# Strassen products for nine pairs of projection units, with GpSimd making the sums

## The chip, the cores and the metric

One core of one Trainium2 chip runs the kernel. The metric is device time in microseconds, the median of the runs. The engines are named as the profile names them: PE (TensorE, matmuls; PEld is its weight load), DVE (VectorE), ACT (ScalarE), POOL (GpSimd) and SP (SyncE, which issues most DMAs). Each engine works through its own instructions in a fixed order, and semaphores hold an instruction until its inputs are there.

## The reference

A decoder layer on 1024 tokens of width 1024, in float32. After a modulated RMS norm, one wide projection feeds a convolution branch and an attention branch.

```python
h = _rmsnorm(x, norm_g[layer]) * (1.0 + scale) + shift
proj = h @ w_in[layer]
(glu_a, glu_b, z_conv, q, k, v, z_att, g_conv, g_att) = jnp.split(proj, split_idx, axis=-1)
u = glu_a * jax.nn.sigmoid(glu_b)
u = lax.conv_general_dilated(u, conv_w...)+ conv_b        # depthwise, causal, 31 taps
u = jax.nn.silu(_layernorm(u, conv_ln_g[layer], conv_ln_b[layer]))
y_conv = (u * jax.nn.silu(z_conv)) @ w_conv_out[layer]
...                                                        # dilated attention on q, k, v
merged = jax.nn.sigmoid(g_conv) * y_conv + jax.nn.sigmoid(g_att) * y_att
x = x + gate * (merged @ w_o[layer])
return _rmsnorm(x, final_g)
```

## The kernel before

Matrices are kept transposed in tiles of 128 channels by 1024 tokens. Every float32 product is made as three matmuls of reduced-precision parts (`mm3`, L73 to L75): a tile is split into a high part, rounded by ScalarE, and a low part, the difference (`split`, L57 and L58). `hh` and `hl` are the two parts of the normed input `h`, resident for the whole projection.

The work goes in stages. A start stage loads and norms, and projects the first `Values` group and three units. Then comes the list `todo`: a `Unit` is one tile of 128 output channels (two halves of 512 tokens, each 8 x 3 matmuls of 128x512 into one PSUM bank), with weights loaded into `wraw` by SP and split into `whi` and `wlo`. A `Values` entry is a group of value columns, as long as four units. Units of the list are the GLU halves of the eight convolution tiles (`Glu(ct)`: sigmoid half, then the half that makes the tile `u`), the SiLU gates `za` of the attention, the SiLU of `z_conv` (kept in the SBUF tiles `z0` to `z7`), and last the eight gate units of the merge (to DRAM).

Beside these matmuls VectorE runs the convolution, one generator `conv(ct, u)` per tile: 31 taps into two accumulators `v` and `v2`, alternately, their sum, and a running sum `tot1` over the tiles. `pump` is a small planner: after each piece of matmuls it hands VectorE as many operations as the piece's cost allows (`PIECE`, `OP`, `HALF`), and `spend` books other VectorE work against it. Outside the two hand-ordered stages (the start and the attention) the framework's scheduler then sets each engine's final order.

At the entry `last_tap` all convolutions must be done (`drain`), and `norm` starts: the mean by a matmul of `tot1` with ones (L534), squares and their sum `tot2`, column sums on TensorE (L127), a row of factors `lrow`, then for each tile the multiplication by `lrow`, SiLU, product with the SiLU of `z`, and the split into `uh` and `ul`. Eight gate units run beside it. Then the output units of the convolution branch (`project` with `uh` and `ul`, L73 `d<-uh,whi`), the attention, the output of attention, and the last projection.

GpSimd does almost nothing until the attention stage, where it makes the low parts of the weights of `q`, `k` and the gates (L58 on POOL).

Of the kernel before, what the change touches and what calls it, by code (L numbers as in the profile page):

```python
# [8 lines left out]
F32 = mybir.dt.float32  # L9
# [7 lines left out]
P = 128  # L17
# [22 lines left out]
def layer(ctx: ExitStack, tc: tile.TileContext, a, out):  # L40
# [58 lines left out]
    bscr = dram.tile([2, 512], F32, name="bscr")  # L99
    cscr = dram.tile([KT, P, S], F32, name="cscr")  # L100
    ascr = dram.tile([KT, P, S], F32, name="ascr")
    gcscr = dram.tile([KT, P, S], F32, name="gcscr")
# [266 lines left out]
    def slot(tag, name, dt=F32, bufs=1):  # L369
        return pb.tile([P, S], dt, name=name, tag=tag, bufs=bufs)  # L370

    def temp(name):
        return slot("tmp", name, bufs=3)

# [20 lines left out]

    tot1 = slot("l0", "tot1")
    v_t = [None] * KT

    def conv(ct, u):
        v = v_t[ct] = slot(f"v{ct}", f"v{ct}")  # L400
        v2 = temp("v2")
        nc.vector.tensor_scalar(v, u[:, 0:S], cw[:, ct, 0:1], cvec[:, 0, ct:ct + 1], op0=mult, op1=add)
        yield HALF
        nc.vector.tensor_scalar(v2, u[:, 1:1 + S], cw[:, ct, 1:2], None, op0=mult)
        yield HALF
        for k in range(2, TAPS):
            d = v2 if k % 2 else v
            nc.vector.scalar_tensor_tensor(d, u[:, k:k + S], cw[:, ct, k:k + 1], d, op0=mult, op1=add)  # L408
            yield OP
        nc.vector.tensor_add(v, v, v2)  # L410
        yield OP
        if ct == 0:
            nc.vector.tensor_copy(tot1, v)
            yield HALF
        else:
            nc.vector.tensor_add(tot1, tot1, v)
            yield OP

# [3 lines left out]
    class Unit:  # L422


        def __init__(self, u, consume, cost=0.0):
            self.u, self.consume, self.cost = u, consume, cost

        def prepare(self):
            spend(OP)
            self.w = weights(a["w_t"][self.u])  # L430

# [14 lines left out]
    class Values:  # L446
# [5 lines left out]
        def prepare(self):  # L452
            self.w = []
            for kp in range(4):
                raw = load_raw(a["w_v"][self.g, kp])
                hi, lo = slot(f"z{kp}", f"vh{kp}", F32R), slot(f"z{4 + kp}", f"vl{kp}", F32R)
                split(hi, lo, raw)
                spend(OP)
                self.w.append((hi, lo))

        def run(self):
            for t in range(8):
# [12 lines left out]
                yield  # L475

    class Glu:

# [3 lines left out]

        def sig(self, half, s, ps):
            if not half:
                self.sb = temp("sigb")
            nc.scalar.activation(self.sb[:, s], ps, AF.Sigmoid)

        def glu(self, half, s, ps):
            if not half:
                self.u = up.tile([P, TAPS - 1 + S], F32, name="u", tag="u", bufs=2)  # L490
                nc.gpsimd.memset(self.u[:, 0:TAPS - 1], 0.0)
            o = TAPS - 1 + half * 512
            nc.vector.tensor_mul(self.u[:, o:o + 512], ps, self.sb[:, s])
            if half:
                behind.append(conv(self.ct, self.u))
# [3 lines left out]

    def to_tile(tiles, n, name, func, make):  # L500
        def consume(half, s, ps):
            if not half:
                tiles[n] = make(name)
            nc.scalar.activation(tiles[n][:, s], ps, func)
        return consume

    sz_t = [None] * KT

    def to_dram(scr, func=AF.Sigmoid):
        def consume(half, s, ps):  # L510
            y = pb.tile([P, 512], F32, name="gs", tag="gs", bufs=2)
            nc.scalar.activation(y, ps, func)
            nc.sync.dma_start(scr[:, s], y)
        return consume

    za = [Unit(40 + j, to_dram(zascr[j], AF.Silu)) for j in range(4)]
    second = Glu(1)
    todo = [second.units()[1], za[0], *Glu(2).units(), Values(1), *Glu(3).units(), *Glu(4).units(), Values(2),
            *Glu(5).units(), *Glu(6).units(), *za[1:], *Glu(7).units()]
    for ct in range(KT):  # L520
        todo.append(Unit(44 + ct, to_tile(sz_t, ct, f"sz{ct}", AF.Silu, lambda n, ct=ct: slot(f"z{ct}", n))))
    last_tap = len(todo)
    for d in range(KT):
        todo.append(Unit(52 + d, to_dram(gcscr[d])))


    ch, cl = [None] * KT, [None] * KT

    def norm():
# [7 lines left out]
        lrow = up.tile([P, TAPS - 1 + S], F32, name="lrow", tag="u", bufs=2)[:, 0:S]  # L537
        tot2 = slot("l0", "tot2")
        for ct in range(KT):
            nc.vector.tensor_sub(v_t[ct], v_t[ct], mean)  # L540
            yield OP
            if ct == 0:
                nc.scalar.activation(tot2, v_t[ct], AF.Square)
            else:
                sq = temp("sq2")
                nc.scalar.activation(sq, v_t[ct], AF.Square)
                nc.vector.tensor_add(tot2, tot2, sq)
                yield OP
# [5 lines left out]
        for half in range(2):  # L554
            half_row(lrow, lcols, half)
        yield PIECE
        for ct in range(KT):
            v = v_t[ct]
            nc.vector.tensor_mul(v, v, lrow)
            yield OP  # L560
            sg_ = temp("sgu")
            nc.scalar.activation(sg_, v, AF.Silu, scale=cvec[:, 1, ct:ct + 1], bias=cvec[:, 2, ct:ct + 1])
            nc.vector.tensor_mul(v, sg_, sz_t[ct])
            yield OP
            hi = slot(f"z{ct}", f"uh{ct}", F32R)
            lo = slot(f"v{ct - 1}" if ct else "l0", f"ul{ct}", F32R)
            split(hi, lo, v)
            yield OP
            ch[ct], cl[ct] = hi, lo

    todo[0].prepare()
    g_ = Glu(0)
# [3 lines left out]
    for n, unit in enumerate(todo):  # L576
        if n + 1 < len(todo):
            todo[n + 1].prepare()
        if n == last_tap:
            drain()  # L580
            behind.append(norm())
        for _ in unit.run():
            pump(PIECE)
    drain()
# [6 lines left out]
    stab = tabs.tile([P, S], F32, name="stab")  # L591
    posi = pb.tile([P, S], I32, name="posi", tag="tmp", bufs=3)
    nc.sync.dma_start(posi, a["positions"].to_broadcast([P, S]))
    n_ = temp("n_")
    nc.vector.tensor_copy(n_, posi)
# [20 lines left out]

    cb = slot(f"v{KT - 1}", "cb")

    def co_load(d):
        sg_ = temp("sgc")  # L620
        nc.sync.dma_start(sg_, gcscr[d])
        return weights(a["w_co"][d]), sg_
# [3 lines left out]
    for d in range(KT):  # L626
# [5 lines left out]
        def gated(half, s, ps):  # L632
            y = pb.tile([P, 512], F32, name="gs", tag="gs", bufs=2)
            nc.vector.tensor_mul(y, ps, sg_[:, s])  # L634
            nc.sync.dma_start(cscr[d][:, s], y)
            if not half:
                modulation(2 * KT + d, gate_c[:, d:d + 1], wa, temp("jk"), cb)

# [652 lines left out]
```

## Time and profile before

| what | us |
|---|---|
| median of 3 runs (1255.39 to 1258.27) | 1258.24 |
| the profiled execution | 1258.8 |
| its span | 1257.0 |
| TensorE busy | 1233.3 |
| VectorE busy | 909.0 |
| ScalarE busy | 511.7 |
| GpSimd busy | 91.5 |

A matmul's record is longer than the step from one to the next, since they are pipelined, so matmul records must not be added up: the step is read from the start times. In the rows of groups, the first number after the bar is the busy time of the group, the second the mean duration of one. In the rows of a timeline, the first number is the start in the span, the second the duration, and "x2" marks two equal neighbours put together.

### The profile page before, as it was taken

How to read it: one execution, taken by the hardware profiler on the slowest of the kernel's cores; microseconds unless marked ns; L12 is line 12 of the kernel's file. 1: busy time of each engine (PE TensorE's matmuls, PEld its weight loads, DVE VectorE, ACT ScalarE, POOL GpSimd, SP SyncE). 2: the span in 40 equal slices, each digit the busy share in tenths (PEclk: the TensorE clock that was granted, in tenths of full speed). 3: DMA queues.
4: the chain of work that ended last, by engine and by line, in shares of the span. 5: the costliest groups of instructions: out<-in, count | busy, mean ns of one | idle time of the engine just before them, and what ended most of it. 6: DMA issues, size and time to landing. Idle time of an engine off the chain costs nothing.

```text
span 1257.0 us, 16947 instructions
## 1 busy us (share of the span) xinstructions
PE 1233.3 (98%) x6208; PEld 1033.5 (82%) x6208; DVE 909.0 (72%) x1496; ACT 511.7 (41%) x1023; POOL 91.5 (7%) x79
## 2 busy tenths in 40 slices
PE   5999999999999999999999999999999999999997
PEld 4877888888888888888888888888888888887886
DVE  6776999999999986873325657777776762448554
ACT  4554202111222135931015656666666665345211
POOL 0000000000000000000031111111111012100000
PEclk9999999999999999999999999999999999999999
DMA  9531311311211112455636555665575563668231
GB/s 362 174 122 59 118 51 59 109 59 51 74 61 51 51 53 82 127 174 193 191 85 150 133 131 145 164 172 144 158 186 146 133 185 120 205 224 294 100 101 67
DMA packets 89751, 165.35 MB, mean 132 GB/s; under 512 B 28547, under 2 KB 42179, under 8 KB 89669
## 3 DMA queue, kind: packets, MB, share of 16 engines
q1 hardware_dynamic: 72992, 157.67, 42.0%
q10 hardware_dynamic: 16676, 6.61, 1.9%
q8 instruction: 49, 0.80, 0.3%
q14 instruction: 34, 0.27, 0.1%
HBM read 105.74 MB, written 27.04 MB: 106 GB/s over the span
## 4 chain that ended last, share of the span: by engine, by line
PE 94%; DMA 2%; DVE 1%; ACT 1%; issue 0%; SPq 0%; ACTq 0%; DVEq 0%
PE d L73 22%; PE d L75 22%; PE d L74 22%; PE o L916 4%; PE t L895 2%; PE d L1195 2%; PE d L1194 2%; PE d L469 2%; PE d L1196 2%; PE d L467 2%; PE d L468 2%; PE s L881 2%; PE s L880 2%; PE d L251 1%; PE d L249 1%; PE d L250 1%
## 5 line engine op out<-in xcount | busy, mean ns | idle before, releaser
L73 PE MATMUL d<-hh,whi 128*128 128x512 f32 x1072 | 421.4, 393 | 0.0
L74 PE MATMUL d<-hl,whi 128*128 128x512 f32 x1072 | 418.4, 390 | 1.9 <-DVE hl L349 1.9
L75 PE MATMUL d<-hh,wlo 128*128 128x512 f32 x1072 | 418.7, 391 | 0.0
L408 DVE SCALAR_TENSOR_TENSOR v<-u,cw,v 128x1024 f32<-128x1024 f32 x232 | 280.6, 1285 | 0.0
L75 PEld LDWEIGHTS d<-hh,wlo 128*128 128x128 f32 x1072 | 201.4, 188 | 42.6
L74 PEld LDWEIGHTS d<-hl,whi 128*128 128x128 f32 x1072 | 201.6, 188 | 41.4 <-DVE hl L349 2.8
L73 PEld LDWEIGHTS d<-hh,whi 128*128 128x128 f32 x1072 | 201.6, 188 | 38.9 <-issue 0.2
L57 ACT ACTIVATE whi<-wraw 128x512 fp32r<-128x512 f32 (+1 forms) x106 | 85.8, 830 | 212.7 <-PE d L74 204.8
L58 POOL TENSOR_TENSOR wlo<-wraw,whi 128x512 fp32r<-128x512 f32 (+1 forms) x56 | 82.1, 1481 | 644.0 <-ACT whi L57 643.9
L884 DVE CUSTOM_DVE_ANT_0 sb<-s,mask 128x128 f32<-128x128 f32 (+1 forms) x192 | 59.9, 350 | 68.3 <-PE s L881 67.7
L888 ACT ACTIVATE sb<-sb,stats 128x128 f32<-128x128 f32 (+1 forms) x192 | 84.9, 444 | 39.0 <-DVE stats L884 38.7
L916 PE MATMUL o<-ph,vt 128*64 128x128 f32 (+1 forms) x432 | 70.9, 270 | 0.0
L895 PE MATMUL t<-ident,sb 128*128 128x128 f32 x280 | 70.8, 274 | 0.0
L58 DVE TENSOR_TENSOR wlo<-wraw,whi 128x1024 fp32r<-128x1024 f32 (+1 forms) x50 | 57.4, 1149 | 14.7 <-ACT whi L57 14.1
L713 ACT ACTIVATE ph<-t 128x384 fp32r<-128x384 f32 (+2 forms) x96 | 45.7, 476 | 37.8 <-PE t L895 31.5
L916 PEld LDWEIGHTS o<-ph,vt 128*64 128x64 f32 x432 | 50.0, 135 | 8.8
L716 DVE TENSOR_TENSOR pl<-t,ph 128x384 fp32r<-128x384 f32 (+2 forms) x96 | 52.0, 542 | 4.2 <-ACT ph L713 3.7
L916 PE MATMUL o<-pl,vt 128*64 128x128 f32 (+1 forms) x216 | 52.9, 261 | 0.0
L1194 PE MATMUL d<-oh,hh 128*128 128x512 f32 (+1 forms) x136 | 51.3, 377 | 0.0
L1196 PE MATMUL d<-oh,hl 128*128 128x512 f32 (+1 forms) x136 | 51.3, 377 | 0.0
L880 PE MATMUL s<-k,q 128*128 128x128 f32 (+1 forms) x192 | 51.1, 291 | 0.0
L634 DVE TENSOR_TENSOR gs<-d,sgc 128x512 f32<-128x512 f32 x16 | 11.1, 692 | 54.9 <-PE d L75 48.9
(227 smaller groups left out, 1909.6 us busy)
## 6 DMA issues: line engine op xcount, KB each, us to landing
wraw<-in_w_t SPq DMA_DIRECT2D x67, 512.0 KB, 3.9
k<-kqp SPq DMA_DIRECT2D x96, 128.0 KB, 2.4
q<-kqp SPq DMA_DIRECT2D x96, 128.0 KB, 2.5
wa<-in_w_ada SPq DMA_DIRECT2D x16, 512.0 KB, 6.6
ql<-kqp SPq DMA_DIRECT2D x48, 128.0 KB, 2.4
wg<-wscr SPq DMA_DIRECT2D x48, 128.0 KB, 3.1
wraw<-in_w_v SPq DMA_DIRECT2D x11, 512.0 KB, 3.6
x<-in_xT SPq DMA_DIRECT2D x8, 512.0 KB, 10.2
```

Of the source, the lines that this page charges most:

```text
L57: nc.scalar.activation(hi, raw, AF.Copy)
L58: (lo_eng or nc.vector).tensor_sub(lo, raw, hi.bitcast(F32))
L73: nc.tensor.matmul(ps, lh, rh, start=start, stop=False)
L74: nc.tensor.matmul(ps, lh, rl, start=False, stop=False)
L75: nc.tensor.matmul(ps, ll, rh, start=False, stop=stop)
L408: nc.vector.scalar_tensor_tensor(d, u[:, k:k + S], cw[:, ct, k:k + 1], d, op0=mult, op1=add)
L880: nc.tensor.matmul(ps[:, c:c + w], q[:, ts_], k[:, ks], start=True, stop=False)
L888: nc.scalar.activation(sb[:, c:c + w], sb[:, c:c + w], AF.Exp, bias=stats[:, t, h, 1:2], scale=-1.0, accum_out=stats[:, t, h, 0:1])
L895: yield from ((lambda c=c: nc.tensor.transpose(ps[:, c:c + P], sb[:, c:c + P], ident)) for c in range(0, o, P))
L916: nc.tensor.matmul(out_, l, r, **kw))
L1194: nc.tensor.matmul(ps, hh[:, k, c], rh, start=k == 0, stop=False)
L1196: nc.tensor.matmul(ps, hl[:, k, c], rh, start=False, stop=k == KT - 1)
```

## The change

Nine times, two units that were made one after the other are made together as a `Pair`. Two units of 128 channels on 1024 tokens with 1024 input channels are a product of 2x2 blocks (input channels in two halves, tokens in two halves, the two units), and Strassen's scheme in Winograd's form makes it with seven block products of 4 x 3 matmuls instead of eight. Four sums of blocks of `h` are needed once (`h_sums`, split into parts, in the SBUF tiles `t0` to `t15`), four sums of weight blocks for each pair, and seven sums of results. GpSimd makes the sums of `h` and of weights and all their low parts, the low parts of `Values` and of the gate units, six low parts of the norm, and the running sum `tot1` for all convolution tiles but the last; VectorE adds the results from PSUM. The first tap of each convolution goes to ScalarE. Convolution tiles that are finished while the sums of `h` occupy SBUF go to DRAM (`put_away`) and come back later (`fetch`); the SiLU of `z_conv` goes to DRAM as well (`szscr`) and is loaded in the norm. The list is in a new order: seven plain units, the nine pairs, then three gates with the two `Values` between them, then `last_tap` and five gates.

```diff
+    def put_away():
+        for ct, v, away in stores:
+            if ct == 0:
+                nc.gpsimd.tensor_copy(tot1, v)
+            else:
+                (nc.gpsimd if ct + 1 < KT else nc.vector).tensor_add(tot1, tot1, v)
+            if away:
+                nc.sync.dma_start(vdr[ct], v)
+                stored.append(ct)
+        stores.clear()
+    def fetch():
+        for ct in stored:
+            v_t[ct] = slot(f"t{8 + ct}", "vb")
+            nc.sync.dma_start(v_t[ct], vdr[ct])
+        stored.clear()
     def conv(ct, u):
-        nc.vector.tensor_scalar(v, u[:, 0:S], cw[:, ct, 0:1], cvec[:, 0, ct:ct + 1], op0=mult, op1=add)
+        nc.scalar.activation(v, u[:, 0:S], AF.Identity, bias=cvec[:, 0, ct:ct + 1], scale=cw[:, ct, 0:1])
         nc.vector.tensor_scalar(v2, u[:, 1:1 + S], cw[:, ct, 1:2], None, op0=mult)
...
         nc.vector.tensor_add(v, v, v2)
-            nc.vector.tensor_add(tot1, tot1, v)
+        stores.append((ct, v, away))
...
     class Values:
-                split(hi, lo, raw)
+                split(hi, lo, raw, nc.gpsimd)
...
+    def h_sums(c):
+        tensor = nc.gpsimd
+        ha, hb = slot("t19", "ha"), slot("t20", "hb")
+        for x, k in ((ha, c), (hb, c + 4)):
+            tensor.tensor_add(x, hh[:, k].bitcast(F32), hl[:, k].bitcast(F32))
+        (a11, a21), (a12, a22) = ((x[:, 0:512], x[:, 512:1024]) for x in (ha, hb))
+        s1, s2, s3, s4 = a22, a11, a21, a12
+        tensor.tensor_add(s1, a21, a22)
+        tensor.tensor_sub(s3, a11, a21)
+        tensor.tensor_sub(s2, s1, a11)
+        tensor.tensor_sub(s4, a12, s2)
+        for i, raw in ((0, s1), (2, s3), (1, s2), (3, s4)):
+            split(sum_tile(i, 0, c), sum_tile(i, 1, c), raw, tensor)
+    class Pair:
+        def prepare(self):
+            tensor = nc.gpsimd
+            ra, rb = (load_raw(a["w_t"][x.u]) for x in self.units)
+            b11, b21, b12, b22 = ra[:, 0:512], ra[:, 512:], rb[:, 0:512], rb[:, 512:]
...
+            split(*w["b11"], b11, tensor)
+            tensor.tensor_sub(t1, b12, b11)
+            tensor.tensor_sub(t3, b22, b12)
+            split(*w["t1"], t1, tensor)
+            tensor.tensor_sub(t2, b22, t1)
+            split(*w["t2"], t2, tensor)
+            split(*w["t3"], t3, tensor)
...
+            split(*w["b21"], b21, tensor)
+            tensor.tensor_sub(t4, b21, t2)
...
+            split(*w["t4"], t4, tensor)
+            split(*w["b22"], b22, tensor)
+        def product(self, ps, name, x):
+            hi, lo = self.w[name]
+            for c in range(4):
...
+                mm3(ps, hi[:, w], lo[:, w], rh, rl, c == 0, c == 3)
+        def run(self):
...
+            nc.scalar.activation(p, product("b11", (0, 0)), AF.Copy)
+            x = product("t2", 2)
+            sums((r, x, p))
+            x = product("t3", 3)
+            sums((q, x, r))
+            x = product("t1", 1)
+            sums((r, x, r))
+            sums((o22, x, q))
+            x = product("b21", (0, 1))
+            sums((p, x, p))
+            one.consume(0, wide(0), p, p)
+            x = product("t4", (1, 1))
+            sums((q, x, q))
+            one.consume(1, wide(1), q, q)
+            x = product("b22", 4)
+            sums((r, x, r))
+            for half, x in ((0, r), (1, o22)):
+                two.consume(half, wide(half), x, x)
...
+gates = [Unit(52 + d, to_dram(gcscr[d]), lo_eng=nc.gpsimd) for d in range(KT)]
+zc = [Unit(44 + ct, to_dram(szscr[ct], AF.Silu)) for ct in range(KT)]
+todo = [second.units()[1], za[0], *Glu(2).units(), *za[1:]]
+for glu, z in ((3, 0), (4, 1), (None, 2), (5, 3), (6, None), (7, None)):
+    if glu:
+        todo.append(Pair(*Glu(glu).units()))
+    if z is not None:
+        todo.append(Pair(*zc[2 * z:2 * z + 2]))
+todo += [gates[0], Values(1), gates[1], Values(2), gates[2]]
 last_tap = len(todo)
+todo += gates[3:]
...
     def norm():
-            split(hi, lo, v)
+            split(hi, lo, v, nc.gpsimd if ct < 6 else None)
...
     for n, unit in enumerate(todo):
+        put_away()
+        if n < 4:
+            h_sums(n)
```

What this does to the order on GpSimd is seen in two pieces. All of GpSimd's work between the start of the projections and the attention was, before, one clearing of the head of `u` per convolution tile; the next row is already the attention's:

```order
L491 MEMSET u 128x30 x8
L58 TENSOR_TENSOR wlo<-wraw,whi 128x8x64 x4
L662 MEMSET ql 64x1024 x3
L670 MEMSET mask 128x256
L671 AFFINE_SELECT mask<-mask 128x128
```

Now 40 operations of `h_sums` stand there first, and then the parts of one pair after another with running sums between them. This is the first pair's piece (`wt` and `wlo` are low parts, L557 to L570 the sums of weight blocks, `tot` the running sum):

```order
L58 TENSOR_TENSOR wt<-wraw,wt 128x512
L647 MEMSET u 128x30
L412 COPY tot_790<-v_850 128x1024
L58 TENSOR_TENSOR wlo<-wraw,whi 128x512
L557 TENSOR_TENSOR wraw<-wraw 128x512
L558 TENSOR_TENSOR wraw<-wraw 128x512
L58 TENSOR_TENSOR wt<-wraw,wt 128x512
L562 TENSOR_TENSOR wraw<-wraw 128x512
L58 TENSOR_TENSOR wt<-wraw,wt 128x512
L570 TENSOR_TENSOR wraw<-wraw 128x512
L58 TENSOR_TENSOR wlo<-wraw,whi 128x512 x4
```

A queue of 158 operations has come to GpSimd ahead of the norm, and a running sum there waits for the last sum of a convolution on VectorE, with the next parts behind it.

On VectorE, before, where the third convolution ends and the fourth begins (L408 are taps, L410 the sum of the two accumulators, L416 the running sum, L402 and L404 the first two taps of the next tile, L493 the product that makes its `u`):

```order
L408 SCALAR_TENSOR_TENSOR v_1388<-u,cw,v_1388 128x1024
L408 SCALAR_TENSOR_TENSOR v_1387<-u,cw,v_1387 128x1024
L402 TENSOR_SCALAR v_1722<-u,cw,cvec 128x1024
L493 TENSOR_TENSOR u<-d,sigb 128x512 x2
L410 TENSOR_TENSOR v_1387<-v_1387,v_1388 128x1024
L404 TENSOR_SCALAR v_1723<-u,cw 128x1024
L416 TENSOR_TENSOR tot_765<-tot_765,v_1387 128x1024
L408 SCALAR_TENSOR_TENSOR v_1722<-u,cw,v_1722 128x1024
```

Now, in the first pair (L601 are the seven sums, with `d` a PSUM bank; L435 and L438 taps; L440 the sum of the two accumulators; L649 the product that makes `u`):

```order
L438 SCALAR_TENSOR_TENSOR v_1196<-u,cw,v_1196 128x1024
L601 TENSOR_TENSOR gs<-d,gs 128x512
L601 TENSOR_TENSOR gs<-d,pq 128x512
L440 TENSOR_TENSOR v_1196<-v_1196,v_1197 128x1024
L601 TENSOR_TENSOR pq<-d,pq 128x512
L431 TENSOR_SCALAR v_1522<-u,cw 128x1024
L435 SCALAR_TENSOR_TENSOR v_1521<-u,cw,v_1521 128x1024
L601 TENSOR_TENSOR pq<-d,pq 128x512
L435 SCALAR_TENSOR_TENSOR v_1522<-u,cw,v_1522 128x1024
L649 TENSOR_TENSOR u<-gs,sigb 128x512
L601 TENSOR_TENSOR gs<-d,gs 128x512
```

The running sum and the first tap have left VectorE's row, as the low parts of the paired units' weights have, and sums that wait for TensorE's products have come in between the taps, in order with them.

180 lines of the change are left out of this document (127 added, 53 removed).

## The prediction

> **What bounds the kernel now.** I read the page's busy times first, then the busy times by stretch, then the chain of work that ended last, then the groups of instructions inside the stretch that the change rewrites, and last the timelines of VectorE and GpSimd where both work.
>
> ```profile
> PE 1233.3 (98%) x6208; PEld 1033.5 (82%) x6208; DVE 909.0 (72%) x1496; ACT 511.7 (41%) x1023; POOL 91.5 (7%) x79
> ...
> core 0: us, PE busy (x) PEld busy (x) DVE busy (x) ACT busy (x) POOL busy (x), PEclk, DMA share, GB/s
> 0.00:101.78 101.78, 86.95 (x376) 68.98 (x377) 70.08 (x97) 53.22 (x56) 0.85 (x7) 1.00 0.59 210
> 101.78:460.56 358.78, 358.78 (x1584) 297.26 (x1583) 353.37 (x312) 72.78 (x94) 4.19 (x8) 1.00 0.20 66
> 460.56:552.37 91.81, 91.81 (x414) 75.68 (x413) 70.51 (x71) 61.14 (x67) 0.00 (x0) 1.00 0.35 111
> 552.37:1257.00 704.63, 695.80 (x3837) 591.53 (x3835) 415.04 (x1017) 324.56 (x807) 86.44 (x64) 1.00 0.56 156
> ```
>
> The four stretches are: the start; the projections with the convolution beside them; the layer norm of the convolution beside the gate units; the rest. TensorE is never idle in the second and third, and its clock is granted in full (1.00). The second holds 1584 matmuls in 358.78 us, 0.2265 us each, and the chain steps in the same beat (a matmul's own record is longer, because they overlap):
>
> ```profile
> 300.05 0.23 PE d L74
> 300.27 0.23 PE d L75
> 300.50 0.23 PE d L73
> ```
>
> But VectorE is busy for 353.37 of those 358.78 us: the two engines are level there, and GpSimd does nothing. What fills VectorE in that stretch, and two rows from later stages that I need for prices:
>
> ```profile
> L408 DVE SCALAR_TENSOR_TENSOR v<-u,cw,v 128x1024 f32<-128x1024 f32 x232 | 280.6, 1285 | 0.0
> L58 DVE TENSOR_TENSOR wlo<-wraw,whi 128x1024 fp32r<-128x1024 f32 x25 | 30.6, 1226 | 2.2 <-ACT whi L57 1.8
> L493 DVE TENSOR_TENSOR u<-d,sigb 128x512 f32<-128x512 f32 x16 | 10.7, 689 | 7.2 <-ACT sigb L486 6.0 <-ACT vh L57 1.1
> L410 DVE TENSOR_TENSOR v<-v,v 128x1024 f32<-128x1024 f32 x8 | 9.8, 1224 | 0.0
> L404 DVE TENSOR_SCALAR v<-u,cw 128x1024 f32<-128x1024 f32 x8 | 6.0, 754 | 0.0
> ...
> L1166 DVE TENSOR_TENSOR sgr<-d,sgr 128x512 f32<-128x512 f32 x16 | 10.6, 686 | 5.4 <-ACT sgr L1151 5.3
> ...
> L562 ACT ACTIVATE sgu<-v,cvec 128x1024 f32<-128x1024 f32 x8 | 9.5, 1238 | 0.1
> ```
>
> The 232 convolution taps alone are 280.6 us, and each reads two SBUF tensors (the input `u` and its own accumulator).
>
> **What VectorE and GpSimd do to each other.** GpSimd works beside VectorE in the attention stage. First GpSimd's rows there, then VectorE's at the same times:
>
> ```profile
> 776.68 2.55 POOL L58 TENSOR_TENSOR wlo<-wraw,whi 128x512 fp32r<-128x512 f32 x2 [14.83 <-ACT whi L57]
> 1006.38 2.38 POOL L58 TENSOR_TENSOR wlo<-wraw,whi 128x1024 fp32r<-128x1024 f32 x1 [17.05 <-ACT whi L57]
> 1087.55 3.04 POOL L58 TENSOR_TENSOR wlo<-wraw,whi 128x1024 fp32r<-128x1024 f32 x1 [8.95 <-ACT whi L57]
> 825.32 2.72 POOL L58 TENSOR_TENSOR wlo<-wraw,whi 128x512 fp32r<-128x512 f32 x2 [11.77 <-ACT whi L57]
> ```
>
> ```profile
> 775.98 0.42 DVE L716 TENSOR_TENSOR vt<-vr,vt 128x256 fp32r<-128x256 f32 x1 [0.25 <-ACT vt L713]
> 777.17 0.87 DVE L943 TENSOR_TENSOR sd<-sd 128x48 f32<-128x48 f32 x1
> 778.08 1.18 DVE L944 TENSOR_TENSOR ma<-sd 128x16 f32<-128x16 f32 x1
> 825.33 0.55 DVE L716 TENSOR_TENSOR pl<-t,ph 128x384 fp32r<-128x384 f32 x1
> 1006.61 2.43 DVE L716 TENSOR_TENSOR vt<-vr,vt 128x256 fp32r<-128x256 f32 x1
> 1087.24 1.08 DVE L979 TENSOR_TENSOR wg<-wg,oc 128x512 f32<-128x512 f32 x1
> 1088.36 2.78 DVE L997 TENSOR_TENSOR wg<-wg 128x512 f32<-128x512 f32 x1
> 1091.18 0.69 DVE L1000 TENSOR_TENSOR wg<-wg,gt 128x512 f32<-128x512 f32 x1
> ```
>
> A product of 128x512 takes 0.69 us at 1091.18; the one at 1088.36 takes 2.78, and ends at 1091.14, 0.55 after the GpSimd operation of 1087.55 (end 1090.59). That operation in its turn began under the VectorE product that ended at 1088.32, and from there on took 2.27 us, as against 2.38 where nothing is in its way. The 0.42 us low part took 2.43 at 1006.61 and ended 0.28 after GpSimd. A sum of 16 columns took 1.18 us beside the second GpSimd operation of 776.68. So an operation of VectorE with two SBUF inputs and one of GpSimd do not run together: whichever came first finishes, the other waits, and they take turns. The low part at 825.33, which reads PSUM and one SBUF tile, took its 0.55 us beside GpSimd: such operations are exempt. The price of a turn is the sum of both, less what overlaps: 2.38 − 2.27 = 0.11 on GpSimd; on VectorE 0.28 instead of the 0.35 that such an operation adds to a busy queue (0.42 less the 0.07 by which a tap's 1.285 us record exceeds its 280.6 / 232 = 1.21), so 0.07. That is 0.18 us a turn.
>
> The Trainium skill, "SBUF — State Buffer", section "SBUF: two separate sides", has this as a rule: VectorE and GpSimd share one port pair as an exclusive lock, taken for the whole instruction by a VectorE operation with two SBUF inputs (or in a two-port mode) or by a GpSimd operation that reads SBUF, and the loser fully blocks. The rows above agree in kind (2.78 us for 0.69); by the rule's whole instructions, without the 0.18 us, the sum below would come to 1452 us, an estimate from that page.
>
> **The change part by part.**
>
> *Matmuls.* Nine pairs, each 7 products of 12 matmuls instead of 96: 9 × 12 = 108 fewer, × 0.2265 = 24.5 us less TensorE work. TensorE alone would reach the mean matmul of the norm (L692) after 7 plain units (336), 9 pairs (756), 3 gates (144), 2 `Values` (384) and 12 more matmuls: 1632 × 0.2265 = 369.6 us, at 471.4.
>
> *VectorE up to there.* 232 taps 280.6; the second tap 6.0; the final sums of two accumulators 9.8; 5 low parts of plain units at 1.22, 6.1; 16 `u` products 10.7; one running sum 1.2; new, 9 × 7 = 63 sums of a product from PSUM with an SBUF tile, at 10.6 / 16 = 0.66 as L1166: 42. Together 356.4 us by group times (the same groups gave 363 before, of which 353.4 were busy time, since neighbours overlap): the first taps (to ScalarE), 28 low parts and 7 running sums go, 63 sums come. VectorE's first operation there comes at about 105. Alone it would end at 461.5, ahead of TensorE.
>
> *GpSimd up to there.* Counted in its new order: 131 operations of 128x512 (32 in the sums of `h`, 99 in the pairs) and 27 of 128x1024 (8 sums of `h`, 7 running sums, 12 low parts of gates and `Values`). At 2.55 / 2 = 1.27 and 2.38: 166.4 + 64.3 = 230.7 us. (The first running sum is a copy; its price is not shown, between the nothing of a copy that locks no one out and 2.38; I take the upper end, since it moves the sum by less than 1%.)
>
> *How they add.* If they exclude each other: 105 + 356.4 + 230.7 = 692. Two things come off. GpSimd can work while VectorE does its 69 operations from PSUM, 46 us; GpSimd is busy for about 40% of the time, so I take 20, bounds 0 and 46. And 158 turns × 0.18 = 28, bounds 0 (no turn contested) and 28. So the convolution's last sum, T, comes at 644, bounds 618 and 692, instead of 460.56. TensorE does not fill that: it is late at once, since the low part of the last plain unit stands 47th in VectorE's row and every row now costs a turn, and in each pair the sums stand in VectorE's row behind 5 to 16 other operations. VectorE is still behind at the end: 84 taps follow the last pair's sum, while TensorE's `Values` and gates (11 units, 120 us) run.
>
> *The norm and the gates behind it.*
>
> ```profile
> 459.33 1.23 DVE L416 TENSOR_TENSOR tot<-tot,v 128x1024 f32<-128x1024 f32 x1
> ...
> 480.85 3.88 DVE L547 TENSOR_TENSOR tot<-tot,sq 128x1024 f32<-128x1024 f32 x3
> ...
> 491.66 0.17 DVE L133 TENSOR_SCALAR lcols<-d 128x8 f32<-128x8 f32 x1 [5.03 <-PE d L127]
> ...
> 496.62 1.23 DVE L559 TENSOR_TENSOR v<-v,lrow 128x1024 f32<-128x1024 f32 x1 [3.42 <-ACT lrow L143]
> ...
> 552.37 0.39 PE L73 MATMUL d<-uh,whi 128*128 128x512 f32 x1
> ```
>
> Before, the first multiplication by the row of factors came 36 us after T, 5 of them a wait for TensorE to reach the column sums. After, TensorE has 60 matmuls (13.6 us) between the mean and the column sums, so it waits there for VectorE and 30 us remain. Behind it stand on VectorE 16 products and two low parts (18 × 1.14, the step between back-to-back ones of 1.22), three operations of the tables (0.7 each) and the low part of the first output weight: 24 us; and 9 GpSimd low parts (6 of the norm, 3 of gates) at 2.38 − 0.18 in turn with them: 20. The first output unit starts at T + 30 + 24 + 20 = T + 74. TensorE's own 168 matmuls behind the column sums end at about T + 67, so that is 7 us of idle TensorE.
>
> *Costed at nothing.* First taps on ScalarE, 8 × 1.24 us, with the extra high parts: ScalarE is busy 72.78 of 358.78 us there; if that cover went, a pair's seven high parts would delay its parts by a few us. The stores of five tiles and of the SiLU of `z`, and their loads: DMA share 0.20 there. A tile's store waits on SP for VectorE's last sum, with the next weight loads behind it; with three raw buffers they are a unit ahead. Running sums wait at GpSimd's head for VectorE; priced in the third rival.
>
> *Sum.* 644 + 74 + 704.6 (unchanged after the first output unit starts) + 1.8 (the profiled execution took 1258.8 for a span of 1257.0) = 1424 us. The profiled execution stands 0.6 us above the median of the runs, 1258.24, so nothing is corrected for that.
>
> **The rivals.** *Taps do not exclude GpSimd (faster).* Every row that shows turns is a sum, difference or product of two tensors; no scalar-tensor-tensor tap meets GpSimd in this trace. If taps are exempt, T is TensorE's 471.4, the output stage starts 67 later, and the time is 471.4 + 67 + 704.6 + 1.8 = 1245. The point at which this decides: the end equals the old one when T = 552.4 − 74 = 478, that is when only 17 of GpSimd's 231 us hold VectorE up. Against it: a tap reads two SBUF tensors like the product at 1088.36.
>
> *Half of GpSimd's work hides.* If turns are contested only for half of it, because GpSimd waits for ScalarE's high parts while VectorE goes on and fills the gaps late, T is about 105 + 356 + 115 = 576, less 20, and the end 1336. Against it: waiting for ScalarE shifts GpSimd's work but does not shorten it, and VectorE has no idle time to give.
>
> *A ring of waits (slower still).* A running sum stands on GpSimd's queue ahead of the next pair's parts and waits for a convolution's last sum; VectorE's next operations in order are sums of a product that TensorE cannot make without those parts. Five such places, each up to a pair's 11 operations (14 us), would add some 70: 1495.
>
> **How the numbers follow.** The forecast has 0.77, taps exempt 0.09, half hidden 0.07, the ring 0.07. The likeliest case's own range runs from 618 + 74 + 706.4 = 1398 to 692 + 74 + 706.4 = 1472; widened by what the hand count of waits may miss, 1360 to 1480 holds eight in ten. A measurement here can tell about 0.3%, 4 us, from no change: faster 0.08 (nearly all of the second case), same 0.01, slower 0.91.
>
> **What the profile after would show.** Taps with a mean well above 1285 ns, near 2.2 us while GpSimd has work, and sums from PSUM still at about 0.69; GpSimd's 128x512 operations above 1.27; VectorE near full from 105 to about 640 and TensorE with idle time there, released by VectorE's low parts and by GpSimd; 108 fewer matmuls at the same 0.2265. Taps that stay at 1285 beside a busy GpSimd would make the prediction wrong.

## The result and the profile after

The changed kernel takes 1401.34 us (median of 4 runs, 1398.5 to 1402.92), beside 1258.26 (1255.39 to 1258.31) of the kernel before: a ratio of 1.114, 95% interval 1.112 to 1.117. It is 143 us slower; the forecast was 1424, with a range of 1360 to 1480.

First the page of the kernel after (busy times; the chain of work that ended last, by engine and by line; two of TensorE's groups), then the busy times by stretch, cut at the same four places as before: the last sum of the convolution now ends at 614.05, and the first output matmul starts at 692.66.

```profile
PE 1254.3 (90%) x6100; PEld 1037.5 (74%) x6100; DVE 1037.7 (74%) x1504; ACT 553.1 (40%) x1101; POOL 459.2 (33%) x247
...
PE 49%; DVE 22%; issue 4%; DMA 1%; ACT 1%; POOL 0%; DVEq 0%; SPq 0%; ACTq 0%; POOLq 0%
DVE v L435 16%; PE d L73 11%; PE d L75 11%; PE d L74 11%; PE o L1096 3%; PE t L1075 2%; PE d L1375 2%; PE d L1376 2%; PE d L1374 2%; PE s L1061 2%; PE s L1060 1%; DVE gs L601 1%; DMA sgr<-ascr 1%; DVE pq L601 1%; DVE tot L705 1%
...
L73 PE MATMUL d<-hh,whi 128*128 128x512 f32 x856 | 343.0, 401 | 26.7 <-ACT whi L57 26.7
...
L73 PE MATMUL d<-s,whi 128*128 128x512 f32 x72 | 35.8, 497 | 36.2 <-ACT whi L57 36.2
```

```profile
core 0: us, PE busy (x) PEld busy (x) DVE busy (x) ACT busy (x) POOL busy (x), PEclk, DMA share, GB/s
0.00:101.30 101.30, 87.70 (x380) 69.68 (x381) 70.07 (x97) 53.73 (x57) 0.85 (x7) 1.00 0.59 214
101.30:614.05 512.75, 405.29 (x1630) 324.06 (x1628) 487.59 (x333) 127.57 (x188) 336.01 (x167) 0.88 0.23 74
614.05:692.66 78.61, 65.33 (x257) 52.45 (x257) 53.40 (x48) 46.02 (x49) 36.67 (x9) 0.86 0.33 108
692.66:1398.10 705.44, 696.00 (x3837) 591.29 (x3835) 426.62 (x1027) 325.76 (x808) 85.64 (x64) 1.00 0.55 157
```

All of the loss lies in the second stretch: 512.75 us instead of 358.78. The third is shorter (78.6 instead of 91.8, with five gates in it instead of eight), the first and the last are what they were. TensorE has its 108 matmuls fewer and now idles, for 107.5 us of this stretch, at a mean granted clock of 0.88; 62.9 us of that were ended by a high part `whi` from ScalarE (the two rows of L73 above). VectorE is busy for 487.59 of the 512.75, with 333 operations for which the prediction counted 356 us. The groups of VectorE and GpSimd show which operations grew (columns as in part 5 of the page; L431 is the second tap, L601 a sum from PSUM, L649 the product `u`, here in its two forms):

```profile
L435 DVE SCALAR_TENSOR_TENSOR v<-u,cw,v 128x1024 f32<-128x1024 f32 x224 | 390.7, 1796 | 1.0 <-ACT v L430 0.7
L431 DVE TENSOR_SCALAR v<-u,cw 128x1024 f32<-128x1024 f32 x8 | 19.2, 2398 | 0.1
L649 DVE TENSOR_TENSOR u<-gs,sigb 128x512 f32<-128x512 f32 x10 | 12.8, 1312 | 0.1
L601 DVE TENSOR_TENSOR gs<-d,gs 128x512 f32<-128x512 f32 x18 | 12.2, 678 | 0.0
...
L649 DVE TENSOR_TENSOR u<-d,sigb 128x512 f32<-128x512 f32 x6 | 3.9, 684 | 9.7 <-ACT sigb L642 9.7
```

```profile
L58 POOL TENSOR_TENSOR wlo<-wraw,whi 128x512 fp32r<-128x512 f32 x36 | 65.9, 1847 | 21.0 <-ACT whi L57 21.0
...
L562 POOL TENSOR_TENSOR wraw<-wraw 128x512 f32<-128x512 f32 x9 | 19.7, 2194 | 0.7
```

A tap has gone from 1285 to 1796 ns. The product `u` takes 1312 ns from two SBUF tiles and 684 where one of them is in PSUM; what reads PSUM stays at 676 to 684. One stretch of the timelines, VectorE's rows and then GpSimd's, shows how:

```profile
129.77 15.63 DVE L435 SCALAR_TENSOR_TENSOR v<-u,cw,v 128x1024 f32<-128x1024 f32 x7
158.24 1.90 DVE L58 TENSOR_TENSOR wlo<-wraw,whi 128x1024 fp32r<-128x1024 f32 x1 [12.84 <-ACT whi L57]
```

```profile
131.06 2.14 POOL L528 TENSOR_TENSOR ha<-ha 128x512 f32<-128x512 f32 x1
133.28 2.15 POOL L529 TENSOR_TENSOR ha<-hb,ha 128x512 f32<-128x512 f32 x1
...
151.31 1.26 POOL L527 TENSOR_TENSOR hb<-ha,hb 128x512 f32<-128x512 f32 x1
```

Seven taps take 15.63 us, 2.23 each, while GpSimd's operations of 1.26 take 2.14: one of each per turn, on both engines alike. At 151 VectorE has nothing to do, and GpSimd is back at 1.26. The bracket at 158.24 shows something the prediction did not have: VectorE stood idle for 12.84 us, waiting for a high part from ScalarE.

### The profile page after: what moved, and what is told of

The parts are those of the page before. It is cut to its first block, busy times and chain, and to the rows that moved or that the text cites. A ratio compares the mean times of both kernels' runs of the same rounds, so it can differ in the third digit from the quotient of the medians.

```text
span 1398.1 us, 17171 instructions
## 1 busy us (share of the span) xinstructions
PE 1254.3 (90%) x6100; PEld 1037.5 (74%) x6100; DVE 1037.7 (74%) x1504; ACT 553.1 (40%) x1101; POOL 459.2 (33%) x247
## 4 chain that ended last, share of the span: by engine, by line
PE 49%; DVE 22%; issue 4%; DMA 1%; ACT 1%; POOL 0%; DVEq 0%; SPq 0%; ACTq 0%; POOLq 0%
DVE v L435 16%; PE d L73 11%; PE d L75 11%; PE d L74 11%; PE o L1096 3%; PE t L1075 2%; PE d L1375 2%; PE d L1376 2%; PE d L1374 2%; PE s L1061 2%; PE s L1060 1%; DVE gs L601 1%; DMA sgr<-ascr 1%; DVE pq L601 1%; DVE tot L705 1%
## 5 line engine op out<-in xcount | busy, mean ns | idle before, releaser
L435 DVE SCALAR_TENSOR_TENSOR v<-u,cw,v 128x1024 f32<-128x1024 f32 x224 | 390.7, 1796 | 1.0 <-ACT v L430 0.7
L73 PE MATMUL d<-hh,whi 128*128 128x512 f32 x856 | 343.0, 401 | 26.7 <-ACT whi L57 26.7
L58 POOL TENSOR_TENSOR wlo<-wraw,whi 128x512 fp32r<-128x512 f32 (+1 forms) x100 | 176.8, 1784 | 539.4 <-ACT whi L57 523.1
L75 PE MATMUL d<-hh,wlo 128*128 128x512 f32 x856 | 339.2, 396 | 13.5 <-DVE wlo L58 7.7
L74 PE MATMUL d<-hl,whi 128*128 128x512 f32 x856 | 338.5, 395 | 1.9 <-DVE hl L351 1.9
L73 PEld LDWEIGHTS d<-hh,whi 128*128 128x128 f32 x856 | 164.1, 192 | 59.0 <-ACT whi L57 27.6
L75 PEld LDWEIGHTS d<-hh,wlo 128*128 128x128 f32 x856 | 163.4, 191 | 51.0 <-DVE wlo L58 9.6
L74 PEld LDWEIGHTS d<-hl,whi 128*128 128x128 f32 x856 | 164.0, 192 | 34.1 <-DVE hl L351 2.8
L73 PE MATMUL d<-s,whi 128*128 128x512 f32 x72 | 35.8, 497 | 36.2 <-ACT whi L57 36.2
L497 PE MATMUL d<-vh,hh 128*128 128x512 f32 x128 | 51.2, 400 | 13.0 <-ACT gs L660 13.0
L58 POOL TENSOR_TENSOR wt<-wraw,wt 128x512 fp32r<-128x512 f32 x27 | 49.5, 1843 | 15.9 <-ACT wt L57 15.9
L498 PE MATMUL d<-vl,hh 128*128 128x512 f32 x128 | 51.2, 400 | 1.8 <-POOL vl L58 1.7
```

Source lines behind the costliest of these rows:

```text
L58: (lo_eng or nc.vector).tensor_sub(lo, raw, hi.bitcast(F32))
L73: nc.tensor.matmul(ps, lh, rh, start=start, stop=False)
L74: nc.tensor.matmul(ps, lh, rl, start=False, stop=False)
L75: nc.tensor.matmul(ps, ll, rh, start=False, stop=stop)
L497: nc.tensor.matmul(ps, hh[:, k, ts_], rh, start=k == 0, stop=False)
```

## The experiments

The theory was that VectorE's and GpSimd's operations with SBUF operands take turns, and that this is the loss. The rivals were that something in the chain GpSimd, ScalarE, TensorE holds the stretch up, whatever VectorE does. In each cut of an edit, "..." stands for lines left out. The kernel before ran beside each group of runs, at 1255.8 to 1257.3 us (medians of 7 runs).

### Turns away: accumulators in PSUM (e1_psum)

```
-        v2 = temp("v2", 1)
+        v_out, v, v2 = v, accp.tile([P, S], F32, name="a1", tag="a1"), accp.tile([P, S], F32, name="a2", tag="a2")
...
-        nc.vector.scalar_tensor_tensor(v, u[:, k:k + S], cw[:, ct, k:k + 1], v, op0=mult, op1=add)
+        nc.vector.scalar_tensor_tensor(v_out, u[:, k:k + S], cw[:, ct, k:k + 1], v, op0=mult, op1=add)
...
+    pd_ctx.close()
+    pd = pd_ctx.enter_context(psum_pool("pdb", bufs=4))
+    accp = pd_ctx.enter_context(psum_pool("acc", bufs=1))
```

> The convolution's two accumulators lie in PSUM (four banks; four are left for the products), so a tap reads one SBUF tile only. GpSimd's 158 operations and the list are as in the changed kernel. If the taps lose their time by taking turns with GpSimd over SBUF: taps go back from 1796 to about 1290 ns, the convolution's last sum comes at 475 to 500 us instead of 614, and the time is 1250 to 1290 us. If the loss is GpSimd's own chain of sums and parts, or a ring of waits between GpSimd, TensorE and VectorE: GpSimd's work is unchanged, and the time stays at 1380 us or more.

It took 1313.41 us (1310.74 to 1314.53; ratio 1.045, 1.043 to 1.046): between the two expectations. Its groups of taps and of GpSimd's low parts, and then the busy times of its stretch up to the last sum (columns as above):

```profile
L435 DVE SCALAR_TENSOR_TENSOR a<-u,cw,a 128x1024 f32<-128x1024 f32 x224 | 272.7, 1280 | 12.9 <-ACT a L430 12.7
...
L58 POOL TENSOR_TENSOR wlo<-wraw,whi 128x512 fp32r<-128x512 f32 x36 | 46.8, 1315 | 32.8 <-ACT whi L57 32.8
```

```profile
101.30:504.02 402.72, 360.16 (x1532) 293.71 (x1533) 355.35 (x333) 123.35 (x182) 232.26 (x166) 0.94 0.27 90
```

With one SBUF operand less a tap takes 1280 ns beside a busy GpSimd, and GpSimd's part 1315 instead of 1847. The same 333 operations of VectorE take 355.35 us instead of 487.59, GpSimd's 232.26 instead of 336.01: the turns that are gone cost 132 us of VectorE's time, and 88 us of the end. (A few are left: the product `u` from two SBUF tiles takes 988 ns here, 679 in e2 below, where GpSimd is idle.) The last sum comes at 504.02, but TensorE reaches the mean only at 526.9, and 56 us over the kernel before are left. So there is a second cause.

### The same work without GpSimd, and GpSimd's help without the pairs (e2_vector, e3_lows)

e2 is the changed kernel with all sums and low parts of the stretch on VectorE; e3 is the kernel before with the low parts of the projection units on GpSimd.

```
-        tensor = nc.gpsimd
+        tensor = nc.vector
...
```

> All sums, low parts and running sums that the changed kernel gives to GpSimd before the attention are made by VectorE. If the two engines take turns: VectorE gets 131 x 0.61 + 27 x 1.15 = 111 us of work and loses 131 us of waits, so the last sum comes near 595 us and the time is 1345 to 1385 us, less than with GpSimd's help. If GpSimd's help is worth its own time (no turns, the loss lies in waits for the chain of parts): 111 us more on the fullest engine, 1470 to 1510 us.

```
         def prepare(self):
-            spend(OP)
-            self.w = weights(a["w_t"][self.u])
+            self.w = weights(a["w_t"][self.u], lo_eng=nc.gpsimd)
```

> The kernel before, with one thing changed: GpSimd makes the low parts of the 33 units of the list (25 before the norm, 8 beside it), no pairs. If the two engines take turns: VectorE is rid of 25 x 1.2 = 30 us before the norm and waits for 25 x (2.38 - 0.23) = 54, and about 7 more beside the norm: 1280 to 1290 us. If they run side by side: VectorE gains 40 us of slack, TensorE is the bound: 1255 to 1260 us, the same as before.

e2 took 1337.72 us (one run): VectorE alone, with 490 operations instead of 333, is 64 us faster than VectorE with GpSimd's help. Its stretch up to the last sum:

```profile
101.30:562.37 461.07, 404.81 (x1640) 323.25 (x1638) 454.44 (x490) 131.51 (x188) 0.93 (x8) 0.93 0.23 82
```

That is even less than the 1345 to 1385 us expected: the added operations cost 99 us (454.44 less e1's 355.35) instead of 111, and VectorE was idle for 7 us instead of 25.

e3 took 1280.76 (1279.7 to 1281.21; ratio 1.019, 1.017 to 1.021): no pair is in it, low parts of 1.2 us each are taken off a full engine and given to an idle one, and it is 23 us slower. Its groups:

```profile
L408 DVE SCALAR_TENSOR_TENSOR v<-u,cw,v 128x1024 f32<-128x1024 f32 x232 | 316.0, 1432 | 0.0
...
L58 POOL TENSOR_TENSOR wlo<-wraw,whi 128x1024 fp32r<-128x1024 f32 x41 | 137.8, 3366 | 425.0 <-ACT whi L57 411.3 <-PE o L915 13.7
```

The taps grew by 35.4 us; the low parts take 3366 ns instead of about 2400. With e1 this shows the turns from both sides: taken away they give back 88 us; brought into the kernel before they cost 23 us, although 30 us of low parts leave VectorE.

### VectorE unloaded (e4_few_taps)

This kernel leaves out 24 of the 31 taps of each tile.

```
-        for k in [k for i in range(2, TAPS - 1, 2) for k in (i + 1, i)]:
+        for k in [k for i in range(2, 6, 2) for k in (i + 1, i)]:
```

> The changed kernel with 7 of the 31 taps of each convolution tile; the other 24 are left out. If the loss is VectorE's turns with GpSimd: VectorE's work before the norm falls to about 125 us, TensorE runs nearly without gaps and the time is 1240 to 1265 us. If GpSimd's chain of sums and parts holds TensorE by itself: TensorE keeps its waits for parts in each pair, and the time stays above 1300 us.

It took 1305.97 us (one run), 49 above the kernel before although VectorE was busy for only 169.6 of the 322 us up to the last sum at 423.3:

```profile
101.30:423.26 321.96, 282.49 (x1194) 228.83 (x1193) 169.59 (x141) 108.92 (x161) 242.70 (x160) 0.93 0.26 92
```

TensorE reached the mean at 521.4, where 471.4 was the count of its matmuls. So the second cause is not the load of VectorE. TensorE's largest gap, 23.6 us at 133, was ended by a high part `whi` from ScalarE. The taps that are left still take turns (1941 ns on average), and GpSimd's sums with them, so VectorE may have a part in the length of this gap: in e1, with next to no turns, the largest early gap is 16.2 us.

### Which wait: two moves that did not help (e5_start, e6_gates, e7_both, e8_after_both)

In e1 ScalarE makes the high parts of the sums of `h`, for which GpSimd's sums must be there, ahead of the next unit's `whi`. e5 writes them one unit later:

```
...
-        if n < 4:
-            h_sums(n)
...
         steps(after, 1 if pair else 3)
+        h_parts(waiting)
+        waiting = h_sums(n) if n < 4 else []
```

> The kernel of e1_psum with one thing changed: the high and low parts of the sums of h are made one unit later, behind the next unit's high parts in ScalarE's queue. If ScalarE's queue, held up by GpSimd's sums, cost e1 its two early idle times of TensorE (16.2 and 3.8 us) and the slow clock behind them, the output begins 20 to 35 us earlier than e1's 608.0 and the time is 1278 to 1294 us (e1: 1313.4). If GpSimd's chain of sums is itself what the pairs wait for, the idle time only moves to the first pair, and the time stays at 1305 or above.

It took 1309.36 us (1308.87 to 1310.65; ratio 1.042, 1.040 to 1.044), 4 below e1, with a gap of 16.5 us still there (16.2 in e1). ScalarE's timeline says why:

```profile
139.39 0.63 ACT L57 ACTIVATE s<-ha 128x512 fp32r<-128x512 f32 x1 [0.71 <-POOL ha L528]
140.74 0.63 ACT L57 ACTIVATE s<-ha 128x512 fp32r<-128x512 f32 x1 [0.71 <-POOL ha L529]
143.18 0.63 ACT L57 ACTIVATE s<-hb 128x512 fp32r<-128x512 f32 x1 [1.81 <-POOL hb L530]
143.71 1.04 ACT L57 ACTIVATE whi<-wraw 128x1024 fp32r<-128x1024 f32 x1
```

The `whi` is still behind three sets of high parts of `s`: outside the stretches that are ordered by hand a scheduler sets each engine's order, and it had put them back. The move was not made, so e5 says nothing on the cause.

e6 moves the three gates that the change had put ahead of the last sum back behind it:

```
-    todo += [gates[0], Values(1), gates[1], Values(2), gates[2]]
+    todo += [Values(1), Values(2)]
     last_tap = len(todo)
-    todo += gates[3:]
+    todo += gates
```

> The kernel of e1_psum with one thing changed: all eight gate units stand behind the convolution's last sum, as in the kernel before, and not three ahead of it. If too few gates beside the norm cost time, TensorE reaches the matmul of the mean at 526.9 - 32.7 = 494, the last sum (504 in e1) now decides, and the output begins at 504 plus 79 to 92, 583 to 596 instead of 608.0: a time of 1288 to 1302 us. If the norm is not short of cover, the same work stands in another order and the time stays within 6 us of e1's 1313.4.

It took 1322.04 us (1318.74 to 1324.79; ratio 1.052, 1.050 to 1.054), 9 above e1 and outside both expectations: the reading falls. The mean did come right behind the last sum (503.4), but the output began at 614.5 instead of 608.0: eight gates are 87 us of TensorE, with 17 us of gaps and a granted clock of 0.89 on top, more than the norm needs. Three gates ahead of the sum fill time in which TensorE waits anyway.

e7 has both edits, e8 has both with the accumulators in SBUF.

> The kernel of e1_psum with both changes (high and low parts of the sums one unit later, all gates behind the last sum). If turns on the SBUF, ScalarE's queue at the start and the missing gates are all there is, the last sum of the convolution ends at 470 to 490, the output begins 80 to 92 later (550 to 582), and the time is that of the kernel before within 1.5%: 1243 to 1277 us. If something else in the pairs costs time, it stays above 1285.

> The changed kernel (accumulators in SBUF) with both changes of e7_both. If the turns are a cause by themselves, VectorE still bounds the stretch: its last sum comes only some 10 to 25 us before the 614 of the changed kernel, the output begins 80 to 92 after it, and the time is 1370 to 1400 us, about 110 to 130 above e7_both. If the late start was what made the turns cost so much, the time falls below 1340.

They took 1322.25 us (1320.49 to 1323.75; ratio 1.052) and 1426.61 (1424.44 to 1430.57; ratio 1.136). Since e5's edit had been put back, both tell only of the gates: no change against e6, and 25 us worse than the changed kernel (e8 lies above both of its expectations). Their difference, 104 us, is once more the price of turns.

### ScalarE's order at the start, by hand (e9_hand, e11_after_hand)

e9 is e5 with ScalarE's instructions of the first seven units kept in their written order; e11 is the changed kernel with the same edit.

```
+    by_hand = 7
+    with tc.manual_schedule(engines={nc.scalar.engine}):
+        for n, unit in enumerate(todo[:by_hand]):
+            turn(n, unit)
...
```

> The kernel of e5_start, with ScalarE's instructions of the seven plain units kept in the order in which they are written (in e5_start they were put back in the old order, so that nothing was undone there). If ScalarE's queue behind GpSimd's sums costs e1 its two early idle times (16.2 and 3.8 us), the slow clock after them and VectorE's idle time there, TensorE shows no gap over 6 us between 105 and 200 us, the last sum of the convolution comes 15 to 30 us before e1's 504, and the time is 1283 to 1299 us (e1: 1313.4). If the sums themselves are what the first pair waits for, the idle time moves to about 185 us and the time stays at 1306 or above.

> The changed kernel (accumulators in SBUF) with only the start of e9_hand: high and low parts of the sums one unit later, and ScalarE's instructions of the seven plain units as written. If turns and ScalarE's wait at the start are causes that add up, VectorE still has to pay all its turns and the last sum comes 10 to 25 us before 614: a time of 1376 to 1392 us (changed kernel: 1401.3). If the turns of the start only take the idle time's place (VectorE and GpSimd then work at the same time where one of them waited before), the time stays at 1395 or above.

e9 took 1293.56 us (1288.83 to 1296.66; ratio 1.028, 1.025 to 1.032): 20 below e1, as expected, with no gap over 3 us between 106 and 200. The last sum came at 490.25, 14 earlier (15 to 30 were expected). So ScalarE's queue, held up by GpSimd's sums, is the second cause: once most turns are gone, its order in these seven units is worth 20 us.

e11 took 1397.4 us (1394.12 to 1400.53; ratio 1.112, 1.109 to 1.114), 4 below the changed kernel with overlapping ranges: the other expectation. Its stretch:

```profile
101.30:607.40 506.10, 405.63 (x1623) 323.14 (x1621) 504.38 (x333) 125.91 (x187) 347.83 (x166) 0.89 0.22 75
```

VectorE's idle time is gone (25.2 us in the changed kernel, 1.7 here), but its busy time has risen from 487.59 to 504.38: where one of the two engines had waited, and the other ran alone at full speed, they now take turns.

### The pairs' buffers (e10_all, e12_ro)

e9 still has a gap of 15.5 us at 394.8, like e1's at 407.7 and the changed kernel's 12.9 at 511.8. ScalarE's rows in e9, then VectorE's, then the matmul that waited:

```profile
408.51 1.21 ACT L430 ACTIVATE a<-u,cvec,cw 128x1024 f32<-128x1024 f32 x1 [34.07 <-DVE v L438]
409.65 1.06 ACT L663 ACTIVATE gs<-d 128x512 f32<-128x512 f32 x2
...
373.64 33.46 DVE L435 SCALAR_TENSOR_TENSOR a<-u,cw,a 128x1024 f32<-128x1024 f32 x28
...
408.52 1.30 DVE L652 TENSOR_TENSOR u<-gs,sigb 128x512 f32<-128x512 f32 x2
...
410.29 0.80 PE L497 MATMUL d<-vh,hh 128*128 128x512 f32 x1 [15.53 <-ACT gs L663]
```

A gate's eviction (L663) needs a `gs` buffer; both hold the last pair's quarters until VectorE makes `u` from them (L652), behind 28 taps. Ahead of it ScalarE's first tap (L430) waits for the accumulator as well. So the banks of the gate's products stay full, and TensorE waits 15.5 us. e10 gives the quarters a tile of their own and puts the first tap on VectorE; e12 does the first alone.

```
-            r = pb.tile([P, 512], F32, name="gs", tag="gs", bufs=2)
+            ro = temp("ro", 1)
+            r, o22 = ro[:, 0:512], ro[:, 512:]
...
-        nc.scalar.activation(v, u[:, 0:S], AF.Identity, bias=cvec[:, 0, ct:ct + 1], scale=cw[:, ct, 0:1])
+        nc.vector.tensor_scalar(v, u[:, 0:S], cw[:, ct, 0:1], cvec[:, 0, ct:ct + 1], op0=mult, op1=add)
```

> The kernel of e9_hand, with the pairs' last two quarters in a tile of their own instead of the two buffers that the gates' results take, and the first tap of each tile on VectorE again (7 more operations of 1.27 us there), so that ScalarE waits for no convolution. If ScalarE's wait behind 28 taps costs e1 the 15.5 us gap at 407.7, this gap is gone, and the time is 8 to 20 us below e9_hand. If VectorE's own work bounds the stretch by then, the gap goes and the time stays within 5 us of e9_hand.

> The kernel of e10_all with the first tap of each tile on ScalarE again, as in the changed kernel; the pairs' last two quarters keep their own tile. If VectorE's own work sets the last sum, 7 operations of 1.27 us less on it bring that sum from 493.4 to about 485 and the time to 1274 to 1283 us. If ScalarE's first taps, which wait for VectorE's accumulators, hold up the evictions behind them, the gap of 15 us near 395 is back and the time is 1288 or above.

e10 took 1285.85 us (1284.59 to 1288.08; ratio 1.024, 1.022 to 1.025), e12 1285.83 (1283.41 to 1293.81; ratio 1.025, 1.021 to 1.029): both 8 below e9, though e12's runs overlap with those of e9, and the gap at 394.8 is gone in both. A smaller one came at 362.5 in e12, 8.4 us, and at 360.5 in e10, 11.9 us, ended by a VectorE sum into the new tile (e9 has 3.5 us there). The first tap need not go to VectorE for that: the buffers are enough (though in e12 the scheduler also placed L430 later among the evictions). e12 falls between its two expectations: its last sum came at 490.55, not at 485. Its stretch, and its two largest waits of VectorE:

```profile
101.30:490.55 389.25, 369.44 (x1588) 302.07 (x1589) 356.68 (x333) 124.94 (x184) 236.82 (x166) 0.98 0.27 95
```

```profile
L435 DVE SCALAR_TENSOR_TENSOR a<-u,cw,a 128x1024 f32<-128x1024 f32 x224 | 273.1, 1280 | 13.1 <-ACT a L430 12.8
L604 DVE TENSOR_TENSOR ro<-d,pq 128x512 f32<-128x512 f32 x18 | 12.2, 679 | 13.4 <-DMA szscr<-ro 13.4
```

There is one tile `ro`, and VectorE waits 13.4 us for the stores from it. It waits another 12.8 us for first taps on ScalarE. 9.8 of them lie at 162, where ScalarE itself had stood idle for 10.5 us for a sum of `h` from GpSimd, with the tap behind the high parts of these sums: the second cause once more, on VectorE's side. In e10, with the first taps on VectorE, this wait is gone, but the taps take 10.7 us there: so moving them made no difference to the time. e12 stays 29 us over the kernel before by the medians, 25 between the profiled spans: its last sum comes 30 later (490.6 instead of 460.6), with VectorE busy for about as long as before (356.7 to 353.4) and idle for 33 us instead of 5, 26 of them in these two waits; from there to the first output matmul it takes 5 us less. No run takes both waits away.

## Why the prediction was right, point by point

**The mechanism.** It stood: taps contested at 2.23 us ("near 2.2"), PSUM sums at 0.68, GpSimd's operations at 2.14. e1, e2 and e3 show the cause and not only the rows. One sign was read wrongly ahead of time: TensorE's idle time was to be ended by VectorE's low parts and by GpSimd. Of its 107.5 us in the stretch, 7.7 ended with a low part of VectorE, 16.6 with one of GpSimd, and 62.9 with a high part of ScalarE, whose own longest waits in the pairs were for GpSimd's sums of weights.

**The work of each engine.** 356.4 us of VectorE and 230.7 of GpSimd were counted; with nearly all turns gone e1 measures 355.35 and 232.26. TensorE's 108 matmuls less are there.

**How they add.** This is the term that was mis-sized: T was put at 105 + 356 + 231 − 48 = 644 and came at 614.05. VectorE waited 487.59 − 355.35 = 132 us in turns and was idle for 21 (25.2 us less the first 4): 105 + 356 + 132 + 21 = 614. So of GpSimd's 232 us, 100 cost VectorE no turn, where 48 were taken. By estimate, 21 of them ran while VectorE was idle, which the sum had at zero on both sides; a turn saves 1.21 + 1.27 − 2.23 = 0.25 us instead of 0.18, which is 40 us instead of 28 for the 158 turns; and the 39 that remain by difference would have lain under VectorE's operations from PSUM, for which 20 was taken from bounds of 0 and 46. The start and end of each record in the trace bear this out: GpSimd's operations lie beside an idle VectorE for 23 us and beside its operations from PSUM for 36. The upper bound was the better guess there: the 20 came from GpSimd's share of the time without turns, about 40%, but with its own waits in turns GpSimd was busy for 336 of 513 us. In all, the turns were put 51 us too high (183 instead of 132) and the idle time of 21 us was left out; T is only 30 us off because the two errors offset each other in part.

**The norm and the rest.** T + 74 was forecast for the first output unit, T + 78.6 measured; 704.6 for the rest, 705.4 measured.

**Costed at nothing.** This step failed, though in the changed kernel it moved the total by about 4 us at most (e11, which mends the start alone). ScalarE was called covered because it is busy for a fifth of the stretch. It was not work that was missing there but a place in the queue: ScalarE serves GpSimd, VectorE and TensorE in one order, and a high part that waits for GpSimd holds up the `whi` behind it. 20 us in e9, and 8 more for the evictions that wait for VectorE. In the changed kernel itself, where VectorE's turns end last, e11 finds 4 us of the first, with overlapping ranges.

**TensorE's rate.** 0.2265 us a matmul was expected throughout. Up to the last sum 1630 matmuls took 405.29 us, 36 more than at that rate, at a granted clock of 0.88. It did not set the end there.

**The rivals.** "Taps exempt" was given 1245. e1 makes them exempt: 1313. The rival's price was wrong, since it let TensorE run without waits. "Half of GpSimd's work hides" would have cost VectorE 95 us, the forecast 183; turns and idle time together took 153. What was held against that rival, that VectorE has no idle time to give, did not hold. The ring of waits through the running sums did not show: GpSimd waited 35 us for them, but VectorE's sums of products (L601) never had to wait for one (0.0 us idle in their row): 17.5 of its 25 us of idle time ended with a high part from ScalarE. A chain of waits through ScalarE showed instead.

**The size of the saving.** In the order in which they were taken away, turns were 88 us, ScalarE's queue at the start 20, the shared buffers 8; some 29 stay in e12, where VectorE waits 13 us for stores and 13 for first taps; how much of the end these cost was not measured. None of these versions beats the kernel before. An estimate says why that is hard: VectorE's own 356 us, begun at 105 and without any wait, end at 461, where the kernel before has its last sum; as long as VectorE keeps the taps, the 24.5 us that TensorE saves shorten nothing ahead of that sum.

## What to carry to other kernels

Before work goes to an idle engine, ask what it shares with the engine that bounds: here 232 us of GpSimd's work cost VectorE 132, and VectorE did all of it alone 64 us faster. The accumulators moved to PSUM took the taps out of the turns, and a tap itself became no longer by it (1280 ns, 1285 before). And an engine that is idle three quarters of the time (ScalarE was busy for 127.6 of 512.8 us) is no cover if its instructions run in order and the first waits for a slow engine: look at what stands behind each wait; but mend it last, since while VectorE's turns ended last it was worth about 4 us.

## What the runs showed of the hardware

A second tap (one SBUF tensor, one column of factors) takes 754 ns before and 742 in e2, where GpSimd is idle, 2398 in the changed kernel beside GpSimd, and 1278 with its result in PSUM (e12): so an operation with a single SBUF tensor can take turns too, which the prediction's own reading, two SBUF inputs, left out.

After an idle stretch TensorE comes back slowly. In the changed kernel, behind a gap of 3.68 us:

```profile
309.85 0.79 PE L73 MATMUL d<-s,whi 128*128 128x512 f32 x1 [3.68 <-ACT whi L57]
310.44 0.63 PE L74 MATMUL d<-s,whi 128*128 128x512 f32 x1
```

Some 12 matmuls follow at such records, most of them 0.43 us apart instead of 0.23, for 6 us; after the gaps of 3.4 us and more in this stretch it was 7 to 14 of them. Two gaps of 2.4 us, each with a second of about 1 us right behind it, were followed by 8 and 10; one of 1.65 us by none. So a wait of 3.4 us or more costs TensorE some 2 to 3 us on top of its length. The Trainium skill, "TensorE: Matmul & The Clock Gate", section "Part 1: The HAM clock gate (the "warmup" mystery)", has an idle window of about 3.4 us bring the clock to half until a busy window has passed; 0.43 against 0.23 and the few microseconds agree.
